# A hybrid decoder layer: conv states as whole tiles, the mLSTM's maps in three fp32r passes, five background steps beside the first norm

## The chip, the cores and the metric

The kernel runs on one core of a Trainium2 chip. The metric is device time in microseconds (us) of one execution. TensorE (PE) does the matrix products, with its weight loads shown apart as PEld; VectorE (DVE), ScalarE (ACT) and GpSimd (POOL) do the rest, and SyncE (SP) issues most of the DMAs. ACT issues some DMAs as well. Each engine works through its own list of instructions in order.

## The reference, cut to what matters

```
z = x @ w_in            # q, k, v, c (mLSTM's q/k path), vm, o, i, f
c_act = silu(causal_conv(c, w_conv, b_conv))             # width 4, depthwise
q = einsum('nlhd,hde->nhle', c_act, w_mq)                # 4 heads of 128: the "maps"
k = einsum('nlhd,hde->nhle', c_act, w_mk) * 128 ** -0.5
att = swa_attend(...)                                    # window 128, sinks, ALiBi
h = mlstm_chunk(C, n, m, q, k, v, logi, logf)            # chunk after chunk of 128 tokens
y = concat([head_norm(att), head_norm(sigmoid(o) * h)])
x1 = layer_norm(ALPHA * x + y @ w_out)                   # the "first norm"
out = layer_norm(ALPHA * x1 + (silu(x1 @ w_gate) * (x1 @ w_up)) @ w_down)
```

There are 2048 prompt tokens with 16 meta tokens ahead of them, and 8 running sequences of 8 tokens (the sample), 2128 columns in all. For the sample the conv begins with three stored columns of each sequence (state_conv, `sconv` in the kernel). The last three c columns of the prompt and of each sequence are outputs (`pconv`, `osconv`). Model width is 1024, and everything is float32.

## The kernel before, in words

Tokens lie along the free axis of a tile and features along the partitions. An accurate product is three fp32r matmuls: a tensor is split into a high part (a cast, `hi_of`, L111) and the rest (a subtraction, L120), and `mm3` multiplies high by high, high by low and low by high (L123, L124, L125). One output tile takes 8 slices of the inner dimension, so 24 matmuls.

Stage 1a (up to about 228 us) makes v, vm, o and the gates. Stage 1b (228 to about 505 us) goes over five groups of columns, `IN_GROUPS`, 426 columns wide (the last one 424). In each group nine weight tiles `m` follow one another: first the four of c, then those of q and k. Three of them (`late`) are left out of the last group and done in stage 2. A c tile is copied to `ext` (L969), the conv runs on ACT and DVE (L923 to L929) and gives `cz`, and four tiles later `maps` multiplies it with two 128x128 matrices (L937); the result goes through `ev` (L939) to FM in DRAM. These L937 matmuls take plain float32 operands. In the last group the sample's columns have a tile `exs` of their own, into which three stored columns are loaded (L973, once a head), and out of which three columns are stored (L976); L975 stores the prompt's three. All of these are issued by ACT.

In the first group the weights of stage 1b come through a raw tile `wbr`, of which there is one, and `mapr` has a tile of its own.

Stage 2 (505 us to the end) takes five groups of `FF_GROUPS` columns: `out_proj` (weights by `wtile`, L1000, three ahead at most; inputs by `load_y`, L1047), `ln1`, then gate, up and down products and the second norm. Ahead of the first group `load_z` (L1058) loads the residual, and the tiles `xr` for the late products come by L1186. The first `ln1` sums squares (L450), forms 1/sqrt on DVE (`rsqrt`, L129 to L136, a chain of small instructions), spreads it by matmul (L462), scales (L1106), and makes the high and low parts of x1 (L1115, L1122).

Attention and mLSTM of the chunks are *background steps*: `bg_step()` takes the next step of a generator, and `pace` spreads steps over the other work. The first norm has 12 steps of its own, behind `mark[7]`, the last L1122 of the norm: `tc.issue_after` keeps their instructions on an engine behind that one in order of issue. The order of instructions within each engine is otherwise decided by a scheduler. PSUM has 3 buffers named `gps` and 5 named `bps`.

Of the kernel before, what the change touches and what calls it, by code (L numbers as in the profile page):

```python
# [9 lines left out]
F32 = mybir.dt.float32  # L10
F32R = mybir.dt.float32r
# [6 lines left out]
KD = 8  # L18
# [31 lines left out]
def tile_hymba(  # L50
# [5 lines left out]
    nc = tc.nc  # L56
    V, A, G, PE, SP = nc.vector, nc.scalar, nc.gpsimd, nc.tensor, nc.sync
# [17 lines left out]
    def gps(shape=None):  # L75
        return pg.tile(shape or [128, 512], F32, tag="g", name="gps")
# [32 lines left out]
    def hi_of(eng, out, src):  # L109
        if eng == "a":  # L110
            A.copy(out, src)  # L111
        elif eng == "p":
            G.tensor_scalar(out=out, in0=src, scalar1=1.0, scalar2=0.0, op0=ALU.mult, op1=ALU.add)
        else:
            V.tensor_copy(out, src)

    def split(eng, hi, lo, src, veng=V):

        hi_of(eng, hi, src)
        return veng.tensor_tensor(out=lo, in0=src, in1=hi.bitcast(F32), op=ALU.subtract)  # L120

    def mm3(out, wh, wl, xh, xl, start, stop):
        PE.matmul(out, lhsT=wh, rhs=xh, start=start, stop=False)  # L123
        PE.matmul(out, lhsT=wh, rhs=xl, start=False, stop=False)  # L124
        PE.matmul(out, lhsT=wl, rhs=xh, start=False, stop=stop)  # L125
# [34 lines left out]
    def load_w(i):  # L160
        m = MT[i]
        if i < NEARLY:
            raw = ep.tile([128, KD, 128], F32, tag="wbr", name="wbr", bufs=1)
            hi, lo = w_tile(), w_tile()
        else:
            raw = b1["w"].tile([128, KD, 128], F32, tag="wbr", name="wbr", bufs=1)
            hi = b1["w"].tile([128, KD, 128], F32R, name=f"wbh{m}")
            lo = b1["w"].tile([128, KD, 128], F32R, name=f"wbl{m}")
        SP.dma_start(out=raw, in_=w1b[:, m, :].rearrange("p (k j) -> p k j", j=128))
        split("p" if i % 2 else "a", hi, lo, raw)  # L170
        wbh[m], wbl[m] = hi, lo
# [10 lines left out]
    with ExitStack() as s1:  # L182
        wp = s1.enter_context(tc.tile_pool(name="w1a", bufs=1, reuse_waits="tile"))
# [44 lines left out]
        start = [[f() for _ in CUT] for f in (gps, bps)]  # L228
# [14 lines left out]
        for i in range(NCH + 1):  # L243
# [11 lines left out]
            else:  # L255
                ps = []
                for c0, w in CUT:
                    xh, xl, n = xs[i]
                    p = (gps if flip[0] % 8 < 3 else bps)()
# [586 lines left out]
    for c in range(NCH):  # L846
        e = P0 + 128 * (c + 1)
# [8 lines left out]
    def bg_step():  # L856
        while done[0] < len(queue) and queue[done[0]][1] <= ready[0]:
            try:
                next(queue[done[0]][3])
                return True  # L860
            except StopIteration:
                done[0] += 1
        return False
# [7 lines left out]
    def steps_to(col):  # L871
        return sum(q[2] for q in queue[done[0]:] if q[0] <= col)
# [31 lines left out]
    with ExitStack() as s1:  # L904
        wp = s1.enter_context(tc.tile_pool(name="w1b", bufs=1, reuse_waits="tile"))
        b1.update(w=wp)
        tp = s1.enter_context(tc.tile_pool(name="t1b", bufs=1, reuse_waits="tile"))
        mapr = wp.tile([128, 8, 128], F32, name="mapr")
        ext = {}
        for g, w in enumerate(IN_GROUPS):  # L910
            c0 = sum(IN_GROUPS[:g])
            wp_ = w if g < 4 else w - NS

            def conv(h):

                e, es = ext[g, h]
                z = tp.tile([128, 426], F32, tag="cz", name="cz", bufs=CZ)
                th = tp.tile([128, 426], F32, tag="ct", name="ct", bufs=1)
                runs = [(z[:, 0:wp_], lambda j: e[:, j:j + wp_])]
                if es is not None:  # L920
                    runs.append((z[:, wp_:w].rearrange("p (n i) -> p n i", i=8), lambda j: es[:, :, j:j + 8]))
                for o, src in runs:
                    A.activation(out=o, in_=src(0), func=AF.Identity, scale=Q[:, Q_WC + 4 * h:Q_WC + 4 * h + 1],  # L923
                                 bias=Q[:, Q_BC + h:Q_BC + h + 1])
                    for j in range(1, 4):
                        V.scalar_tensor_tensor(out=o, in0=src(j), scalar=Q[:, Q_WC + 4 * h + j:Q_WC + 4 * h + j + 1],
                                               in1=o, op0=ALU.mult, op1=ALU.add)
                A.activation(out=th[:, 0:w], in_=z[:, 0:w], func=AF.Tanh, scale=0.5)
                V.scalar_tensor_tensor(out=z[:, 0:w], in0=th[:, 0:w], scalar=1.0, in1=z[:, 0:w],  # L929
                                       op0=ALU.add, op1=ALU.mult)  # L930
                return z

            def maps(h, cc):
                for j in range(2):
                    p = gps()
                    m = 4 * j + h
                    PE.matmul(p[:, 0:w], lhsT=mapr[:, m, :], rhs=cc[:, 0:w], start=True, stop=True)  # L937
                    ev = tp.tile([128, 426], F32, tag="ev", name="ev", bufs=4)
                    A.activation(out=ev[:, 0:w], in_=p[:, 0:w], func=AF.Copy,  # L939
                                 scale=0.5 if j == 0 else 0.5 * 128.0 ** -0.5)  # L940
                    A.dma_start(out=FM[:, 5 + 4 * j + h, c0:c0 + w], in_=ev[:, 0:w])

            conved = {}
            for idx, m in enumerate(MT[:NMT[g]]):
                if g == 0 and NEARLY <= idx + 3 < len(MT):
                    load_w(idx + 3)
                if g == 0 and idx == 3:
                    SP.dma_start(out=mapr, in_=wmap)
                if g == 1 and idx == 3:
                    with tc.issue_after(xdma[0].ins):  # L950
                        SP.dma_start(out=skT[:, :, 0:120], in_=ckT[:, :, 8:128])
                        SP.dma_start(out=sv[0:120], in_=cv[8:128])
                if g == 0 and idx == 2:
                    gates()
                p = gps()
                for k in range(KD):
                    xh, xl = xg[g, k]
                    mm3(p[:, 0:w], wbh[m][:, k, :], wbl[m][:, k, :], xh[:, 0:w], xl[:, 0:w], k == 0, k == KD - 1)
                if m < 5:
                    out_q(tp, p, m, c0, w)  # L960
                else:
                    h = m - 5
                    e = tp.tile([128, 429], F32, tag="ext", name="ext", bufs=5)
                    if g == 0:
                        V.memset(e[:, 0:3], 0.0)
                    else:
                        pw = IN_GROUPS[g - 1]
                        V.tensor_copy(e[:, 0:3], ext[g - 1, h][0][:, pw:pw + 3])
                    A.copy(e[:, 3:3 + wp_], p[:, 0:wp_])  # L969
                    es = None  # L970
                    if g == 4:
                        es = tp.tile([128, 8, 11], F32, tag="exs", name="exs", bufs=4)
                        A.dma_start(out=es[:, :, 0:3], in_=sconv[:, h])  # L973
                        A.copy(es[:, :, 3:11], p[:, wp_:w].rearrange("p (n i) -> p n i", i=8))
                        A.dma_start(out=pconv[:, h, :], in_=e[:, wp_:wp_ + 3])  # L975
                        A.dma_start(out=osconv[:, h], in_=es[:, :, 8:11])  # L976
                    ext[g, h] = (e, es)
                    conved[h] = conv(h)
                if idx - MDLY in conved:
                    maps(idx - MDLY, conved.pop(idx - MDLY))  # L980
                left = sum(NMT[g:]) - LEFT - idx
                if g > 0:
                    pace(steps_to(need(0)) / max(left, 1.0))
            for h in sorted(conved):
                maps(h, conved.pop(h))
            if g + 1 < 5:
                for k in range(KD):
                    load_xg(g + 1, k)
            ready[0] = c0 + w if g < 4 else c0
            if g == 0:  # L990
                early.close()
                bp = ctx.enter_context(tc.tile_pool(name="bg", bufs=1, side="right", reuse_waits="tile"))


    with ExitStack() as s2:
# [184 lines left out]
        cl, wl_ = sum(IN_GROUPS[:4]), IN_GROUPS[4]  # L1180
# [12 lines left out]
        mark = {7: None}  # L1193
        for _ in ln1(z, FF_GROUPS[0], s0, x1, True, mark):
            pass
        for m in late:
            h, l = wnext()
            p = bps()
# [1 line left out]
                mm3(p[:, 0:wl_], h[:, k, :], l[:, k, :], xq[k][0][:, 0:wl_], xq[k][1][:, 0:wl_], k == 0, k == KD - 1)  # L1200
            out_q(None, p, m, cl, wl_)
        ready[0] = T
        with tc.issue_after(mark[7]):
            for _ in range(12):
                bg_step()
        pend = None
        for g in range(NG):
            w = FF_GROUPS[g]
# [161 lines left out]
```

## Time and profile before

| | |
|---|---|
| three runs | 2504.2, 2506.12, 2508.94 us (median 2506.12) |
| the profiled execution | 2508.94 us, of which the span of its instructions is 2507.1 us |
| PE busy | 98% of the span |
| DVE, ACT, POOL busy | 60%, 38%, 13% |
| DMA | 327.89 MB, 197330 packets, of them 31010 under 512 B |

The page cuts the span in 40 slices of 63 us and gives the busy share of each engine in tenths. PE is at 9 in all but four of them, and its granted clock at 9 (90% or more of full speed) in all but two. Such a view shows which engine bounds the whole; the few places at which PE stands still are seen in the timeline alone.

### The profile page before, as it was taken

The page shows a single profiled execution, that of the slowest core. Times are in us where ns is not written, and L with a number is a line of the kernel's source. Part 1 is how long each engine was busy: PE and PEld are TensorE (multiplying, and loading weights), DVE is VectorE, ACT ScalarE, POOL GpSimd, SP SyncE. Part 2 cuts the span into 40 slices and gives each one's busy share as a digit, 9 for nine tenths or more (in the row PEclk, how much of TensorE's full clock was granted, in tenths as well). Part 3 has the DMA queues.
Part 4 walks back from the last instruction along what each step waited for, and adds up shares of the span by engine and source line. Part 5 has one row for each costly group of instructions (what it writes and reads, how often), then busy time and mean ns, then how long its engine had stood idle before and what let it go on. Part 6 is the DMA issues. An engine that isn't in the chain of part 4 may idle for free.

```text
span 2507.1 us, 34929 instructions
## 1 busy us (share of the span) xinstructions
PE 2444.7 (98%) x13135; PEld 2267.2 (90%) x13135; DVE 1514.9 (60%) x3129; ACT 955.3 (38%) x1730; POOL 328.3 (13%) x253
## 2 busy tenths in 40 slices
PE   8999999889999999999999999999999999999997
PEld 8999888788989989888999899989899999999997
DVE  6214466457786888656674976666775434764444
ACT  3112444335433444324333543343343323443332
POOL 1000000021000014210011500100420000420001
PEclk9999999998999999999999999999999999999998
DMA  7222534563444543554343353433344333343342
GB/s 234 89 90 85 173 119 131 132 207 117 144 130 126 160 146 94 175 159 144 120 137 121 106 188 122 140 119 107 109 142 133 117 111 121 104 143 114 118 127 77
DMA packets 197330, 327.89 MB, mean 131 GB/s; under 512 B 31010, under 2 KB 133498, under 8 KB 197146
## 3 DMA queue, kind: packets, MB, share of 16 engines
q1 hardware_dynamic: 170400, 294.29, 38.7%
q10 hardware_dynamic: 26762, 31.36, 3.6%
q8 instruction: 104, 1.70, 0.3%
q14 instruction: 64, 0.52, 0.1%
HBM read 281.59 MB, written 44.99 MB: 130 GB/s over the span
## 4 chain that ended last, share of the span: by engine, by line
PE 88%; DVE 4%; DMA 4%; ACT 1%; issue 1%; POOL 0%; SPq 0%; ACTq 0%; DVEq 0%; POOLq 0%
PE gps L123 25%; PE gps L125 24%; PE gps L124 24%; PE bps L123 2%; PE bps L125 2%; PE bps L124 2%; DMA w<-in_wo 1%; PE bps L513 1%; PE bps L549 1%; PE bps L542 1%; PE gps L937 1%; DVE w L120 1%; PE bps L682 1%; PE bps L655 1%; PE bps L672 1%
## 5 line engine op out<-in xcount | busy, mean ns | idle before, releaser
L123 PE MATMUL gps<-x,w 128*128 128x440 f32 (+4 forms) x2240 | 792.3, 358 | 11.1 <-DVE z L1075 5.6
L125 PE MATMUL gps<-x,w 128*128 128x440 f32 (+4 forms) x2240 | 797.9, 357 | 3.4 <-POOL w L120 2.7
L124 PE MATMUL gps<-x,w 128*128 128x440 f32 (+4 forms) x2240 | 794.0, 356 | 0.6 <-DVE x L1122 0.6
L111 ACT CAST w<-w 128x1024 fp32r<-128x1024 f32 (+2 forms) x423 | 400.6, 947 | 775.2 <-DMA w<-in_wd 271.8
L120 DVE TENSOR_TENSOR w<-w 128x1024 fp32r<-128x1024 f32 (+2 forms) x391 | 441.5, 1130 | 359.7 <-ACT w L111 185.4
L123 PEld LDWEIGHTS gps<-x,w 128*128 128x128 f32 x2240 | 422.4, 189 | 36.5 <-DVE z L1075 7.4
L125 PEld LDWEIGHTS gps<-x,w 128*128 128x128 f32 x2240 | 422.6, 189 | 23.3 <-POOL w L120 4.4
L124 PEld LDWEIGHTS gps<-x,w 128*128 128x128 f32 x2240 | 422.6, 189 | 18.4 <-DVE x L1122 0.9
L123 PE MATMUL gps<-hh,w 128*128 128x440 f32 (+2 forms) x880 | 314.8, 362 | 1.4 <-DVE z L1172 1.3
L125 PE MATMUL gps<-hh,w 128*128 128x440 f32 (+2 forms) x880 | 313.1, 357 | 0.0
L124 PE MATMUL gps<-hl,w 128*128 128x440 f32 (+2 forms) x880 | 312.5, 356 | 0.0
L123 PEld LDWEIGHTS gps<-hh,w 128*128 128x128 f32 x880 | 166.1, 189 | 11.9 <-issue 4.6
L124 PEld LDWEIGHTS gps<-hl,w 128*128 128x128 f32 x880 | 166.3, 189 | 8.1 <-issue 1.5
L125 PEld LDWEIGHTS gps<-hh,w 128*128 128x128 f32 x880 | 166.1, 189 | 7.4 <-issue 0.5
L120 POOL TENSOR_TENSOR w<-w 128x1024 fp32r<-128x1024 f32 x32 | 77.4, 2419 | 727.1 <-ACT w L111 475.2
L1172 DVE SCALAR_TENSOR_TENSOR z<-z,gps 128x440 f32<-128x440 f32 (+2 forms) x160 | 93.0, 589 | 69.1 <-PE gps L125 68.7
L111 ACT CAST hh<-hr 128x440 fp32r<-128x440 f32 (+2 forms) x110 | 60.0, 545 | 165.2 <-DVE hr L1158 165.0
L1158 DVE SCALAR_TENSOR_TENSOR hr<-ft,gps 128x440 f32<-128x440 f32 (+2 forms) x110 | 64.9, 590 | 81.3 <-PE gps L125 81.0
L1155 ACT ACTIVATE ft<-gps 128x440 f32<-128x440 f32 (+2 forms) x110 | 57.4, 522 | 113.1 <-PE gps L125 112.6
L120 DVE TENSOR_TENSOR hl<-hr,hh 128x440 fp32r<-128x440 f32 (+2 forms) x110 | 83.8, 762 | 27.6 <-ACT hh L111 27.3
L1066 POOL TENSOR_TENSOR zs<-zs,z 128x440 f32<-128x440 f32 (+2 forms) x58 | 80.0, 1379 | 102.0 <-DVE z L1075 66.3
L1156 DVE SCALAR_TENSOR_TENSOR ft<-ft,gps 128x440 f32<-128x440 f32 (+2 forms) x110 | 64.7, 588 | 46.4 <-ACT ft L1155 46.3
(338 smaller groups left out, 3111.0 us busy)
## 6 DMA issues: line engine op xcount, KB each, us to landing
w<-in_wg SPq DMA_DIRECT2D x110, 512.0 KB, 3.5
w<-in_wu SPq DMA_DIRECT2D x110, 512.0 KB, 3.5
w<-in_wd SPq DMA_DIRECT2D x80, 384.0 KB, 3.1
w<-in_wd SPq DMA_DIRECT2D x80, 320.0 KB, 2.9
w<-in_wo SPq DMA_DIRECT2D x40, 512.0 KB, 3.7
FM<-ev ACTq DMA_DIRECT2D x52, 213.0 KB, 1.9
TM<-st ACTq DMA_DIRECT2D x16, 578.0 KB, 3.7
vmo<-TM SPq DMA_DIRECT2D x16, 514.0 KB, 3.4
```

The costliest lines, as they stand in the source:

```text
L111: A.copy(out, src)
L120: return veng.tensor_tensor(out=lo, in0=src, in1=hi.bitcast(F32), op=ALU.subtract)
L123: PE.matmul(out, lhsT=wh, rhs=xh, start=start, stop=False)
L124: PE.matmul(out, lhsT=wh, rhs=xl, start=False, stop=False)
L125: PE.matmul(out, lhsT=wl, rhs=xh, start=False, stop=stop)
L513: PE.matmul(s[g][:, j, 0:nk], lhsT=x[r, 2 * tt + j, :], rhs=y[r, 0:nk], start=(i == 0), stop=(i == 2))
L542: PE.transpose(pt[0:n, 128 * t:128 * t + 128], Pt[:, 4 * g + t, c0:c0 + n], ident)
L1066: G.tensor_tensor(out=s[:, 0:w], in0=s[:, 0:w], in1=z[m][:, 0:w], op=ALU.add)
L1155: A.activation(out=t[:, 0:w], in_=pgt[:, 0:w], func=AF.Tanh, scale=0.5)
L1156: V.scalar_tensor_tensor(out=t[:, 0:w], in0=t[:, 0:w], scalar=1.0, in1=pgt[:, 0:w], op0=ALU.add, op1=ALU.mult)
L1158: V.scalar_tensor_tensor(out=hr[:, 0:w], in0=t[:, 0:w], scalar=0.5, in1=pu[:, 0:w], op0=ALU.mult, op1=ALU.mult)
L1172: V.scalar_tensor_tensor(out=zm, in0=zm, scalar=ALPHA if s == 0 else 1.0, in1=p[:, 0:w], op0=ALU.mult, op1=ALU.add)
```

## The change

1. *Conv states.* The four loads of `sconv` become one DMA into a tile `cvi` (issued by SP in group 1), and the sample's and the prompt's last columns are gathered by DVE copies in `cvo` and `cvp`, which two SP DMAs store after the last head. Twelve DVE copies are added; twelve ACT DMAs go, three SP DMAs come.
2. *Maps.* `mapr` is loaded through the shared raw tile and split in `maph` and `mapl`; `cz` is split in two tiles `cs` (three buffers for all), and `mm3` replaces the plain matmul. `ct` has two buffers.
3. *Background steps.* Five of the 12 steps at the first norm are no longer kept behind `mark[7]`.
4. A scratch size of the DMA's is set when the program is made.

```
-        mapr = wp.tile([128, 8, 128], F32, name="mapr")
+        maph = wp.tile([128, 8, 128], F32R, name="maph")
+        mapl = wp.tile([128, 8, 128], F32R, name="mapl")
+        cvi = tp.tile([128, 4, 8, 3], F32, name="cvi")
+        cvo = tp.tile([128, 4, 8, 3], F32, name="cvo")
+        cvp = tp.tile([128, 4, 3], F32, name="cvp")
...
-                th = tp.tile([128, 426], F32, tag="ct", name="ct", bufs=1)
+                th = tp.tile([128, 426], F32, tag="ct", name="ct", bufs=2)
...
+                ch, cl = (tp.tile([128, 426], F32R, tag="cs", name="cs", bufs=3) for _ in range(2))
+                split("a", ch[:, 0:w], cl[:, 0:w], cc[:, 0:w])
...
-                    PE.matmul(p[:, 0:w], lhsT=mapr[:, m, :], rhs=cc[:, 0:w], start=True, stop=True)
+                    mm3(p[:, 0:w], maph[:, m, :], mapl[:, m, :], ch[:, 0:w], cl[:, 0:w], True, True)
...
                 if g == 0 and idx == 3:
+                    mapr = wp.tile([128, KD, 128], F32, tag="wbr", name="mapr", bufs=1)
                     SP.dma_start(out=mapr, in_=wmap)
+                    split("a", maph, mapl, mapr)
                 if g == 1 and idx == 3:
                     with tc.issue_after(xdma[0].ins):
+                        SP.dma_start(out=cvi, in_=sconv)
...
-                        A.dma_start(out=es[:, :, 0:3], in_=sconv[:, h])
+                        V.tensor_copy(es[:, :, 0:3], cvi[:, h])
                         A.copy(es[:, :, 3:11], p[:, wp_:w].rearrange("p (n i) -> p n i", i=8))
-                        A.dma_start(out=pconv[:, h, :], in_=e[:, wp_:wp_ + 3])
-                        A.dma_start(out=osconv[:, h], in_=es[:, :, 8:11])
+                        V.tensor_copy(cvp[:, h, :], e[:, wp_:wp_ + 3])
+                        V.tensor_copy(cvo[:, h], es[:, :, 8:11])
+                        if h == 3:
+                            SP.dma_start(out=pconv, in_=cvp)
+                            SP.dma_start(out=osconv, in_=cvo)
...
-        with tc.issue_after(mark[7]):
-            for _ in range(12):
+        for i in range(12):
+            if i < 5:
                 bg_step()
+            else:
+                with tc.issue_after(mark[7]):
+                    bg_step()
```

The line numbers of the changed kernel are 13 higher from stage 2 on: L1000 is L1013 there, L1047 is L1060, L1058 is L1071, L1106 is L1119, L1122 is L1135, L1186 is L1199.

SP's list around the start of out_proj (`in_wo` are its weights, YD its inputs, `z` and `xr` the loads named above). Before:

```order
L1047 DMA x<-YD 128x384 x2
L1000 DMA w<-in_wo 128x1024
L1047 DMA x<-YD 128x384
L1000 DMA w<-in_wo 128x1024 x2
...
L1058 DMA z<-in_xT 128x384 x5
L1186 DMA xr<-in_xT 128x424
L1058 DMA z<-in_xT 128x440 x5
L1000 DMA w<-in_wo 128x1024
```

And of the change:

```order
L1013 DMA w<-in_wo 128x1024
L988 DMA out_pconv<-cvp 128x12
L1013 DMA w<-in_wo 128x1024
L989 DMA out_osconv<-cvo 128x96
...
L1071 DMA z<-in_xT 128x384 x4
L1071 DMA z<-in_xT 128x440
L1199 DMA xr<-in_xT 128x424
L1013 DMA w<-in_wo 128x1024
L1071 DMA z<-in_xT 128x440 x5
```

The two stores of conv states now stand between the second, the third and the fourth of the weight loads, and the fifth weight load has one of the next group's `z` loads (440 wide) right ahead of it instead of five.

DVE's list in the first norm, from the instruction that starts the 1/sqrt (L455) to the one that ends it. Before:

```order
L455 TENSOR_SCALAR rs<-gps 128x3
L129 TENSOR_SCALAR rs<-rs 128x3
L131 TENSOR_SCALAR rs<-rs 128x3
L120 TENSOR_TENSOR w<-w 128x1024
L134 TENSOR_TENSOR rs<-rs 128x3
```

And of the change (L518 and L523 are attention's scores and their maximum, L676 is the mLSTM's state):

```order
L455 TENSOR_SCALAR rs<-gps 128x3
L120 TENSOR_TENSOR w<-w 128x1024
L518 ISA P,mx<-bps,C,R 128x256
...
L131 TENSOR_SCALAR rs<-rs 128x3
L523 TENSOR_SCALAR mx<-mx 128x8
L524 TENSOR_TENSOR mx<-R,mx 128x8
L134 TENSOR_TENSOR rs<-rs 128x3
...
L676 SCALAR_TENSOR_TENSOR S<-S,DEC,bps 128x129
```

Four L518, L523, L524, two L676 and a copy (L572) have moved in between the steps of the 1/sqrt; before, all of them stood behind the last L1122. On PE the list has changed too, ahead of L462:

```order
L450 MATMUL gps<-avg,sq 128x1 x5
L513 MATMUL bps<-kt,qt 128x256 x2
L672 MATMUL bps<-wkv,ktm 128x129 x2
L682 MATMUL bps<-S,qs 128x129
L683 MATMUL bps<-vmo,gm 128x129
L682 MATMUL bps<-S,qs 128x129
L683 MATMUL bps<-vmo,gm 128x129
L462 MATMUL gps<-C,rs 128x128 x3
```

Before, L462 stood right behind the five L450; the attention and mLSTM matmuls between them came later.

## Rows read from the trace of the kernel before

**Rows 1.** The page: engines' share of the span, and the chain that ended last.

```profile
PE 2444.7 (98%) x13135; PEld 2267.2 (90%) x13135; DVE 1514.9 (60%) x3129; ACT 955.3 (38%) x1730; POOL 328.3 (13%) x253
...
PE 88%; DVE 4%; DMA 4%; ACT 1%; issue 1%; POOL 0%; SPq 0%; ACTq 0%; DVEq 0%; POOLq 0%
```

**Rows 2.** Windows: length; PE, PEld, DVE, ACT, POOL busy; granted clock, DMA share, GB/s.

```profile
300.00:450.00 150.00, 150.00 (x814) 129.02 (x813) 105.41 (x310) 72.87 (x181) 5.79 (x6) 1.00 0.39 122
486.00:498.20 12.20, 5.97 (x24) 5.75 (x25) 3.69 (x7) 4.42 (x8) 0.00 (x0) 0.72 0.84 113
522.00:531.00 9.00, 6.33 (x28) 5.70 (x27) 3.94 (x5) 4.48 (x6) 1.38 (x2) 0.81 0.79 301
561.00:579.00 18.00, 10.55 (x45) 9.29 (x44) 12.97 (x37) 12.19 (x21) 4.03 (x4) 0.62 0.12 41
```

**Rows 3.** Timeline of PE around one pair of maps in group 1: start, duration, what.

```profile
306.16 0.36 PE L123 MATMUL gps<-x,wbh 128*128 128x426 f32 x1
...
307.14 0.36 PE L125 MATMUL gps<-x,wbl 128*128 128x426 f32 x1
307.33 1.59 PE L937 MATMUL gps<-cz,mapr 128*128 128x426 f32 x4
...
308.96 0.36 PE L124 MATMUL gps<-x,wbh 128*128 128x426 f32 x1
```

**Rows 4.** Groups of instructions in stage 1b: busy, mean ns of one, idle before.

```profile
L111 ACT CAST x<-x 128x426 fp32r<-128x426 f32 x21 | 11.3, 548 | 21.9 <-DMA x<-in_xT 17.1 <-DMA FM<-ev 4.3 <-ACT ev L887 0.4
...
L120 DVE TENSOR_TENSOR x<-x 128x426 fp32r<-128x426 f32 x22 | 13.0, 600 | 28.4 <-ACT x L111 14.4 <-PE gps L124 13.9
```

**Rows 5.** Timeline of ACT and PE in group 0.

```profile
241.26 1.05 ACT L111 CAST wbh<-wbr 128x1024 fp32r<-128x1024 f32 x1 [0.79 <-DMA wbr<-in_w1b]
...
251.16 1.59 PE L937 MATMUL gps<-cz,mapr 128*128 128x426 f32 x4
...
253.19 1.05 ACT L111 CAST wbh<-wbr 128x1024 fp32r<-128x1024 f32 x1 [0.25 <-DMA wbr<-in_w1b]
```

**Rows 6.** DMA from 470 to 500 us: packets, and issues (median us to landing).

```profile
DMA packets 5917, 3.04 MB, mean 101 GB/s; under 512 B 4856, under 2 KB 5410, under 8 KB 5916
...
w<-in_wo SPq DMA_DIRECT2D x4, 512.0 KB, 18.5
```

**Rows 7.** The page: the same weight load over the whole run.

```profile
w<-in_wo SPq DMA_DIRECT2D x40, 512.0 KB, 3.7
```

**Rows 8.** Timeline, ACT and PE, end of stage 1b (brackets: idle, releaser).

```profile
490.62 1.04 ACT L111 CAST w<-w 128x1024 fp32r<-128x1024 f32 x1 [6.95 <-DMA w<-in_wo]
...
492.23 0.72 PE L123 MATMUL gps<-x,wbh 128*128 128x424 f32 x1 [6.81 <-ACT ev L887]
...
498.21 1.59 PE L937 MATMUL gps<-cz,mapr 128*128 128x424 f32 x4
...
504.47 0.66 PE L123 MATMUL gps<-x,w 128*128 128x384 f32 x1
```

**Rows 9.** Timeline of SP and PE in the first out_proj; its chain.

```profile
515.28 2.38 SPq L1058 DMA_DIRECT2D z<-in_xT  x5
...
517.80 5.99 DMA w<-in_wo
...
524.97 0.44 PE L123 MATMUL gps<-x,w 128*128 128x384 f32 x1 [2.03 <-ACT w L111]
```

**Rows 10.** Timeline of DVE and PE in the first norm.

```profile
562.05 0.16 DVE L455 TENSOR_SCALAR rs<-gps 128x3 f32<-128x3 f32 x1 [1.42 <-PE gps L450]
...
565.45 1.65 PE L462 MATMUL gps<-C,rs 128*128 128x128 f32 x6 [3.44 <-DVE rs L136]
...
575.99 0.48 DVE L518 CUSTOM_DVE_ANT_0 P<-bps,C,R 128x256 f32<-128x256 f32 x1
...
576.39 0.48 DVE L518 CUSTOM_DVE_ANT_0 P<-bps,C,R 128x256 f32<-128x256 f32 x1
...
581.38 0.61 DVE L676 SCALAR_TENSOR_TENSOR S<-S,DEC,bps 128x129 f32<-128x129 f32 x2 [2.61 <-PE bps L672]
```

More of the change, by code (lines that the diff above doesn't have):

```diff
@@ L1336 @@
     from concourse.bass_utils import run_bass_kernel_spmd as _run
-    nc = _bacc.Bacc("TRN2", target_bir_lowering=False, num_devices=1)
+    nc = _bacc.Bacc("TRN2", target_bir_lowering=False, num_devices=1, dynamic_dma_scratch_size=1024)
     lay = _layout(inputs)
```

## The prediction

> **What bounds the kernel now.** I read the page first: PE is busy in 98% of the span and holds 88% of the chain that ended last, DMA and DVE 4% each [rows 1]. So there are two ways to be faster: less work on PE, or fewer of the places at which PE stands still or runs at a low clock. Work added on another engine costs something only where it makes PE wait.
>
> The windows show where that is [rows 2]. From 300 to 450 us PE is busy for all of 150.00 us at clock 1.00, while DVE has 105.41 and ACT 72.87 of 150: the loop over groups is bound by PE alone. From 486 to 498.2 us PE is busy for 5.97 of 12.20 us at a granted clock of 0.72; from 522 to 531 us for 6.33 of 9 at 0.81; in the first norm, from 561 to 579 us, for 10.55 of 18 at 0.62. A mean under 1 is time at 1.2 GHz instead of 2.4, and it comes here behind PE's idle time each time.
>
> The timeline then says what PE waited for. At 492.23 us it had been idle for 6.81 us, and the releaser is an ACT eviction [rows 8]. But ACT itself had been idle for 6.95 us in front of a weight cast at 490.62 that waited for a load of out_proj's weights: ACT works in order, and the eviction stood behind that cast. So the wait is a late DMA. The DMA view of 470 to 500 us shows how late: four such loads took 18.5 us in the median to land, against 3.7 us for the 40 of the whole run [rows 6, 7]. In the same 30 us 5917 packets moved only 3.04 MB, and 4856 of them were under 512 B [rows 6]. These are the conv states' stores, 12 bytes a run.
>
> **The change part by part.** The sum is made against the profiled execution, 2508.94 us (span 2507.1 and 1.84 around it). It is the slowest of the three runs; the median, 2506.12, is 2.82 lower.
>
> *A. Maps on PE.* A matmul of 426 columns issues every (307.14 - 306.16)/5 = 0.196 us [rows 3]. From 307.14 to 308.96 lie one matmul, the pair of maps (four records) and one more matmul: 1.82 - 2 x 0.196 = 1.43 us for the pair. Six fp32r matmuls in its place take 1.18, which saves 0.25. Groups 0 to 3 have 16 pairs: -4.1 us; the last group is counted in C. The bounds are -2 (each set of three starts with a hand-over that costs half the saving) and -4.1.
>
> The Trainium skill ("FP8 and Floating Point Precision", section "TensorE Precision Notes") says that true FP32 takes four passes through the array. By that a pair would hold eight passes, 1.57 us by the step above, and A would be -6.3. The trace differs, 1.43 us, and decides.
>
> The split adds on ACT a cast of 0.55 us and on DVE a subtraction of 0.60 us for each of 20 heads [rows 4]. Four of each in a group of about 48 us are hidden by idle time: DVE has 44.6 us of 150 free there, ACT 77 [rows 2]. Without that cover it would be at most 20 x 0.60 = 12 us.
>
> *B. Group 0.* `mapr` now takes a turn in the raw weight tile. From the cast at 241.26 to that at 253.19 there are two turns [rows 5], 6.0 us each. The maps' weights take the turn after 241.26: cast at 247.2, low part 2.3 us later (1.05 and about 1.2), ready at 249.5, and the first map stands at 251.16. That is a margin of 1.7 us. The weights behind it come 6 us later and are needed later still. What can stick is the order on DVE: the gates' small chain now stands behind a subtraction that waits for a buffer, and PE has a matmul of that chain behind the first maps. Bounds: 0, and 3 us (two subtractions and a pair, 2 x 0.60 + 1.18, with hand-overs). I take +1.5.
>
> *C. End of stage 1b.* If the twelve ACT DMAs are why the weights are late, PE loses neither the 6.81 us [rows 8] nor the half-rate stretch behind it: 24 matmuls took 498.21 - 492.23 = 5.98 us instead of 4.70. That is -8.1. The last three pairs of maps took 504.47 - 498.21 = 6.26 us [rows 8]. Afterwards they take 3 x (1.18 + 0.60 and a hand-over of some 0.2) = 5.9, since with three `cs` buffers a head's subtraction waits for the maps of the head before: -0.4. On the other side ACT does four casts of 0.55 there that it did not do, in front of evictions that PE waits for, and the third weight load now stands on SP behind the prompt's store, which waits for the last head's copies, so that its cast (1.05) comes among the evictions as well: +3.3 if none of it is hidden. I take -5. Bounds: -2 (the loads come only some us sooner) and -8.5.
>
> The skill speaks against this part in one point: "DMA: Bandwidth & Descriptors", section "Specifications", wants at least 512 B in a transfer for full rate, with a read-modify-write below that, and the whole-tile stores still have only 48 and 384 B a partition. By it they stay slow, and C would be nearer to its -2. The trace agrees that such packets are slow together (101 GB/s in the 30 us above), and no run here shows what one costs.
>
> *D. First out_proj.* The fifth weight load is issued at 517.80, right behind five `z` loads of the next group that take SP 2.38 us [rows 9], and lands 5.99 later (3.7 in the median [rows 7]). PE idles 2.03 us for it [rows 9], and in the 9 us from 522 it idles 2.67 in all at a clock of 0.81 [rows 2], another (1 - 0.81) x 9 = 1.7 us: 4.4. With one `z` load ahead instead of five it is issued 4/5 x 2.38 = 1.9 earlier, and with less traffic up to 2.3 us sooner to land. I take -3.5; bounds 0 (other transfers fill the gap) and -4.4.
>
> *E. First norm.* PE idles 3.44 us in front of L462, during the 1/sqrt [rows 10]. DVE's steps between L455 and its end now have four L518 (0.40 apart), two L676 (0.61 together [rows 10]) and three small ones of about 0.15 among them: 1.6 + 0.61 + 0.45 = 2.7 us later. PE fills some of that with matmuls that it would do later, and the work moved comes off the stretch behind. Bounds: -1 and +4 (the eight L532 ahead of the last L1122, too). I take +1.5.
>
> The single loads of `sconv` delay nothing on PE today, and of the second half of stage 2 only the order changes: 0, and 2 either way.
>
> Sum: -4.1 + 1.5 - 5 - 3.5 + 1.5 = -9.6. That is 2499.3 by the profiled execution and **2496.5 us** by the median.
>
> **The rivals.**
>
> 1. *The waits go almost whole.* The loads land in 4 us, ACT's casts hide, the norm costs nothing: -4.1 + 0.5 - 8.5 - 4.4 + 0 = -16.5, 2489.6. For it speaks that ACT is idle for 6.95 us in front of that cast; against it, that ACT's and SP's order get longer by the change itself.
> 2. *The late weights do not come from the small packets.* Twice 512 KB of weights, inputs and residual are loaded at that time too, and the DMA share stands at 0.84 [rows 2]. If that volume is what holds the loads, C and D are -1 together, and -4.1 + 1.5 - 1 + 1.5 = -2.1: 2504, the same within what can be measured. Against it: 3.04 MB in 30 us is 101 GB/s [rows 6], while from 522 to 531 us the same engines move 301 [rows 2].
> 3. *Slower: DVE stands behind PE.* DVE works in order, and a head's subtraction may wait until PE has done the maps before. A weight tile takes 24 x 0.196 = 4.7 us, of which DVE has about 30% free, 1.4 us. A wait beyond 1.4 us makes the next conv or input split late, and then PE stands. With a wait of 2.4 us at 16 heads: +16 - 9.6, 2512.5; it decides from a wait of about 2 us on (+9.6). Against it: the maps of two heads lie a whole weight tile apart in groups 0 to 3, so the buffer is free long before.
> 4. *The norm takes it.* The 1/sqrt and what follows come 2.7 later, PE's clock stays low longer, and it costs +6 instead of +1.5: 2501, faster by the bound still, but barely.
>
> **How the numbers follow.** Chances: the forecast 0.46 (2492 to 2501), rival 1 0.18, rival 2 0.18, rival 3 0.09, rival 4 0.09. A measurement of this kernel tells about 0.2%, 5 us, from no change, so *faster* is under 2501.1 and *slower* over 2511.1. Faster: 0.46 x 0.95 + 0.18 + half of rival 4 + a little of rival 2 = 0.44 + 0.18 + 0.05 + 0.04, about 0.71. Slower: most of rival 3 and a part of rival 2, 0.09. Same: 0.20. The range goes from 2487 (rival 1 with 3 us more) to 2507 (rival 2 with 3 more); it leaves out rival 3 and the edges.
>
> **What would show it.** A: a pair of maps in group 1 takes about 1.2 us between the matmuls around it. B: PE shows no idle time over 1 us before 300 us. C: the weight loads between 470 and 500 us land in about 4 to 6 us, the idle time of 6.81 is gone, and out_proj starts about 7.6 us earlier than at 504.47 (A, B and C). D: in the first out_proj no wait of PE for a weight over 1 us, clock 1.00. E: L462 begins about 6 instead of 3.4 us after L455. I am wrong if the loads still take over 10 us without the small packets, if DVE shows idle time in front of the subtractions of `cs` in groups 1 to 3 with PE idle behind it, or if later stages lose what these stretches win.

## The result, and the profile after

The change takes 2493.93 us in the median of five runs (2491.22 to 2495.77) against 2508.94 for the kernel before beside it (2504.2 to 2512.17): a ratio of 0.9947, 95% interval [0.9935, 0.9960]. By the ratio it is faster by some 13 us. The time lies within the stated range, 2.6 us under the forecast; the sum of -9.6 came to -13.1 between the two profiled executions, but two terms of that size are in it that the sum did not have.

The page of the change:

```profile
span 2494.0 us, 35048 instructions
PE 2438.8 (98%) x13175; PEld 2271.9 (91%) x13175; DVE 1519.9 (61%) x3162; ACT 965.2 (39%) x1751; POOL 331.5 (13%) x253
...
DMA packets 188866, 327.88 MB, mean 131 GB/s; under 512 B 22546, under 2 KB 125034, under 8 KB 188682
...
w<-in_wo SPq DMA_DIRECT2D x40, 512.0 KB, 3.8
```

PE is as busy a share of the span as before [rows 1], with 5.9 us less work in it. There are 8464 packets fewer for the same bytes.

The DMA view from 470 to 500 us, to be read beside [rows 6]:

```profile
DMA packets 3354, 5.80 MB, mean 193 GB/s; under 512 B 621, under 2 KB 2840, under 8 KB 3352
...
w<-in_wo SPq DMA_DIRECT2D x4, 512.0 KB, 4.6
...
out_osconv<-cvo SPq DMA_DIRECT2D x1, 48.0 KB
out_pconv<-cvp SPq DMA_DIRECT2D x1, 6.0 KB, 2.1
```

621 packets under 512 B instead of 4856, 193 GB/s instead of 101, and the weights land in 4.6 us instead of 18.5. PE's timeline at the end of stage 1b, to be read beside [rows 8]:

```profile
483.84 0.46 PE L123 MATMUL gps<-x,wbh 128*128 128x424 f32 x1 [0.32 <-ACT ev L887]
...
490.57 0.88 PE L123 MATMUL gps<-cs,maph 128*128 128x424 f32 x2 [1.07 <-ACT ev L946]
...
495.16 0.66 PE L123 MATMUL gps<-cs,maph 128*128 128x424 f32 x2 [0.67 <-ACT cs L111]
...
496.67 0.33 PE L123 MATMUL gps<-x,w 128*128 128x384 f32 x1
```

Idle times of 0.32, 1.07 and 0.67 us (and two under 0.4) stand where 6.81 stood, and the first matmul of out_proj (the last row) comes at 496.67 instead of 504.47. ACT's timeline shows what the 1.07 is:

```profile
488.26 0.51 ACT L111 CAST x<-x 128x384 fp32r<-128x384 f32 x1
489.05 1.05 ACT L111 CAST w<-w 128x1024 fp32r<-128x1024 f32 x1 [0.27 <-DVE cz L934]
490.00 0.94 ACT L946 ACTIVATE ev<-gps 128x424 f32<-128x424 f32 x2
```

PE waits there for an eviction (L946), and that stands on ACT behind a weight cast of 1.05 us.

A set of three passes in group 1 looks like this on PE:

```profile
315.95 0.36 PE L123 MATMUL gps<-cs,maph 128*128 128x426 f32 x1
...
316.93 0.36 PE L125 MATMUL gps<-cs,mapl 128*128 128x426 f32 x1
```

Six matmuls issue from 315.95 to 316.93 + 0.20, 1.18 us, as the sum had it against the 1.43 of the pair [rows 3].

In the first out_proj, PE and then SP:

```profile
519.61 0.45 PE L125 MATMUL gps<-x,w 128*128 128x384 f32 x1 [1.06 <-DVE w L120]
```

```profile
505.62 0.33 SPq L1013 DMA_DIRECT2D w<-in_wo  x1
...
511.62 0.33 SPq L1013 DMA_DIRECT2D w<-in_wo  x1
```

The fifth weight load is issued at 505.62, 8.95 us after out_proj began, against 13.33 before (517.80 [rows 9] less 504.47 [rows 8]). PE no longer waits for it, but for the sixth, 1.06 us, and its clock stays at 1.00.

The first norm, DVE and then PE, beside [rows 10]:

```profile
549.96 0.16 DVE L455 TENSOR_SCALAR rs<-gps 128x3 f32<-128x3 f32 x1 [3.11 <-PE gps L450]
...
551.21 0.48 DVE L518 CUSTOM_DVE_ANT_0 P<-bps,C,R 128x256 f32<-128x256 f32 x1
...
553.64 0.34 DVE L676 SCALAR_TENSOR_TENSOR S<-S,DEC,bps 128x129 f32<-128x129 f32 x1
...
555.01 0.16 DVE L136 SCALAR_TENSOR_TENSOR rs<-rs 128x3 f32<-128x3 f32 x1
```

```profile
552.64 0.71 PE L672 MATMUL bps<-wkv,ktm 128*128 128x129 f32 x4 [2.40 <-DVE mx L518]
...
555.22 1.63 PE L462 MATMUL gps<-C,rs 128*128 128x128 f32 x6 [0.21 <-DVE rs L136]
...
561.33 0.66 PE L123 MATMUL gps<-x,w 128*128 128x384 f32 x1 [2.50 <-DVE z L1119]
```

From L455 to L462 it is 5.26 us instead of 3.40. PE fills part of that with the matmuls that were moved (the row of 552.64 is one), but waits 2.40 us for L518 to free a buffer.

Cut at events that both traces have, the span comes apart as follows (the first matmul of the maps, the last group's first, the first of out_proj, the mean of the sums L1085 or L1098 as the norm begins, L462, and the same mean in the next group). The last column is a second profile of the change, taken later, less the same profile of before:

| stretch | before | after | difference | my terms | again |
|---|---|---|---|---|---|
| start to the first map | 251.16 | 251.42 | +0.26 | 0 | +0.52 |
| to the first map of the last group | 232.67 | 231.55 | -1.12 | A, B: -2.6 | -1.25 |
| to out_proj | 20.64 | 13.70 | -6.94 | C: -5 | -5.58 |
| first out_proj | 39.87 | 35.80 | -4.07 | D: -3.5 | -3.32 |
| to L462 | 21.11 | 22.75 | +1.64 | E: +1.5, with the next row | +1.91 |
| L462 to the next group's norm | 391.90 | 382.21 | -9.69 | | -11.47 |
| to the end of the span | 1549.75 | 1556.57 | +6.82 | 0 | +3.89 |

The cuts that no row shown so far has are these, of before:

```profile
483.83 1.58 PE L937 MATMUL gps<-cz,mapr 128*128 128x424 f32 x4
...
544.34 0.81 PE L1085 MATMUL gps<-zs,avg 128*128 128x384 f32 x2
...
957.35 0.90 PE L1085 MATMUL gps<-zs,avg 128*128 128x440 f32 x2
```

and of the change:

```profile
251.42 0.36 PE L123 MATMUL gps<-cs,maph 128*128 128x426 f32 x1
...
482.97 0.55 PE L123 MATMUL gps<-cs,maph 128*128 128x424 f32 x2
...
532.47 0.81 PE L1098 MATMUL gps<-zs,avg 128*128 128x384 f32 x2
...
937.43 0.90 PE L1098 MATMUL gps<-zs,avg 128*128 128x440 f32 x2
```

Up to L462 the differences add up to -10.2, near the -9.6 of the forecast. What I had not seen is the stretch behind it, and that the rest of the kernel can take 7 us more or less.

### The profile page after: what moved, and what is told of

The parts are those of the page before. It is cut to its first block, busy times and chain, and to the rows that moved or that the text cites. A ratio compares the mean times of both kernels' runs of the same rounds, so it can differ in the third digit from the quotient of the medians.

```text
span 2494.0 us, 35048 instructions
## 1 busy us (share of the span) xinstructions
PE 2438.8 (98%) x13175; PEld 2271.9 (91%) x13175; DVE 1519.9 (61%) x3162; ACT 965.2 (39%) x1751; POOL 331.5 (13%) x253
## 4 chain that ended last, share of the span: by engine, by line
PE 86%; DVE 6%; DMA 4%; ACT 1%; issue 1%; POOL 0%; SPq 0%; ACTq 0%; DVEq 0%
PE gps L123 24%; PE gps L124 24%; PE gps L125 24%; PE bps L123 2%; PE bps L125 2%; PE bps L124 2%; PE bps L513 1%; PE bps L549 1%; PE bps L542 1%; DVE w L120 1%; DMA w<-in_wo 1%; DMA w<-in_wd 1%; DMA out_oS<-P 1%; PE bps L655 1%; PE bps L682 1%
## 5 line engine op out<-in xcount | busy, mean ns | idle before, releaser
L120 DVE TENSOR_TENSOR w<-w 128x1024 fp32r<-128x1024 f32 (+2 forms) x391 | 442.4, 1132 | 352.1 <-ACT w L111 175.3
L120 POOL TENSOR_TENSOR w<-w 128x1024 fp32r<-128x1024 f32 x32 | 77.0, 2407 | 765.2 <-ACT w L111 620.2
L120 DVE TENSOR_TENSOR hl<-hr,hh 128x440 fp32r<-128x440 f32 (+2 forms) x110 | 82.9, 754 | 30.8 <-ACT hh L111 30.4
```

## The experiments

All were timed in five rounds or more; ratios are to the kernel before on the same chip, with 95% intervals. Theory: the small packets of `osconv` hold the weight loads, and that is most of it. Rivals: the volume that is loaded there anyway; the number and the place of the DMAs on ACT's list; the maps or the steps as the source of the gain.

### One part at a time

*Conv states alone:* the kernel before with the edits to `cvi`, `cvp` and `cvo` alone, `mapr` and its matmul as before.

> Only the conv states as whole tiles (part 1); maps and background steps as before. Packets theory: the weight loads at 470 to 500 us land in about 5 us instead of 18.5, PE's idle time of 6.8 us is gone, out_proj starts about 7 us earlier, and the time falls by 6 to 9 us. Volume theory: the loads still land after 10 us or more, and the time stays within 2 us. The five z loads still stand ahead of the fifth weight load here, so if their order is what made PE wait in the first out_proj, that wait of about 2 us stays.

2499.18 us, ratio 0.9957 [0.9943, 0.9971]. The DMA view from 470 to 500 us:

```profile
DMA packets 2598, 4.70 MB, mean 157 GB/s; under 512 B 537, under 2 KB 2084, under 8 KB 2596
...
w<-in_wo SPq DMA_DIRECT2D x4, 512.0 KB, 4.6
```

The packets theory agrees: 4.6 us to landing. (Twelve ACT DMAs are gone here as well; the next part separates the two.) From the last group's first map to out_proj it takes 10.98 us, a gain of 9.7. In the first out_proj the wait for the fifth weight shrinks from 2.03 to 1.00 us although the five `z` loads are still ahead of it, so their order is at most half of that wait; in later kernels with the same order it is 0.32 us (the stores without gaps) and none (those and the steps), apart from some 0.65 for that weight's low part, which all of these have.

*Maps alone:* `maph`, `mapl`, `cs` and `mm3`, conv states and steps as before.

> Only the maps in three fp32r passes (part 2); conv states and background steps as before. By the matmul steps: 16 pairs at 0.25 us saved and 1 to 1.5 us lost in group 0, so -2 to -4 us, with the late weights still there (18 us to landing, PE idle 5 to 7 us near 490 us). If the splits on ACT and DVE cost PE something, 0 or slower.

2516.06 us, ratio 1.0022 [1.0013, 1.0031]: slower. The miss is mine: with the late weights still there (15.4 us to landing), the last group's first map to out_proj takes 22.60 us instead of 20.64, and PE waits 2.41 us right ahead of it. In stage 1b it waits 8.1 us in three pieces, 4.9 the longest, for the eviction L887 on ACT, and 3.8 in two for the casts of `cs`.

*Steps alone:*

```
-        with tc.issue_after(mark[7]):
-            for _ in range(12):
+        for i in range(12):
+            if i < 5:
                 bg_step()
+            else:
+                with tc.issue_after(mark[7]):
+                    bg_step()
```

> Only the five background steps moved ahead (part 3). My step E: 1/sqrt of the first norm takes 2.7 us longer, +1.5 us on the whole. Rival: the work moved comes off a later stretch, where the profile of the change has PE idle 2.7 us less and no low clock between 733 and 761 us, so -4 to -8 us.

2507.72 us, ratio 0.9987 [0.9978, 0.9995]. The rival is nearer, but by less than it said: the norm up to L462 takes 25.09 us (+4.0), and from L462 to the next group's norm 381.17 (-10.7).

### Packets, or the number of DMAs

*Each head's store from a tile without gaps.* As many DMAs, by the same engine, in the same places:

```
-                        A.dma_start(out=osconv[:, h], in_=es[:, :, 8:11])
+                        co = tp.tile([128, 8, 3], F32, tag="co", name="co", bufs=4)
+                        V.tensor_copy(co, es[:, :, 8:11])
+                        A.dma_start(out=osconv[:, h], in_=co)
```

> The kernel before with as many DMAs from the same engine, but each head's osconv goes through a DVE copy into a tile without gaps: 96 bytes a partition instead of eight runs of 12, so 512 packets instead of 4096 for the four heads. If the number of packets delays the weights: landing falls from 18.5 to under 8 us, PE's idle time near 490 us falls by 4 us or more, -5 to -8 us. If the number of DMAs or their place on ACT's list does it, or the volume: within 2 us of before.

2496.86 us, ratio 0.9950 [0.9938, 0.9963]: this edit of three lines gives about all that the whole change gives. (Like the change, it sets the DMA's scratch size, as do all kernels here but that of the steps alone. The maps alone have this setting and the old stores, and the weights still take 15.4 us there, so it is not the cause.) The same view:

```profile
DMA packets 4219, 5.81 MB, mean 194 GB/s; under 512 B 1486, under 2 KB 3705, under 8 KB 4217
...
w<-in_wo SPq DMA_DIRECT2D x4, 512.0 KB, 5.0
...
out_pconv<-ext ACTq DMA_DIRECT2D x4, 1.5 KB, 4.0
out_osconv<-co ACTq DMA_DIRECT2D x4, 12.0 KB, 3.5
```

*Half of it:* the same for heads 1 and 3 alone.

> As e4_packets, but only for heads 1 and 3; heads 0 and 2 still store eight runs of 12 bytes a partition, so 2304 packets from osconv instead of 4096 (512 in e4_packets), with as many DMAs. If the delay grows with the packets that stand ahead of the weights: landing of the weights 8 to 13 us, PE idle 1 to 4 us near 490 us, -6 to -11 us. If a few such stores suffice to block: as before. If half of them is harmless: as e4_packets, -13.

2500.86 us, ratio 0.9984 [0.9974, 0.9993]. DMA, then PE:

```profile
DMA packets 5333, 4.82 MB, mean 161 GB/s; under 512 B 3199, under 2 KB 4819, under 8 KB 5331
...
w<-in_wo SPq DMA_DIRECT2D x4, 512.0 KB, 9.4
```

```profile
488.54 0.46 PE L123 MATMUL gps<-x,wbh 128*128 128x424 f32 x1 [2.41 <-ACT ev L887]
```

4096, 2304 and 512 packets of `osconv` give 18.5, 9.4 and 5.0 us to landing, and 6.81, 2.41 and 0 us of PE's idle time in front of that m tile. The other two profiles with 4096 packets have 13.1 (the steps alone) and 15.4 us (the maps alone) to landing. The delay grows with the packets. From the last group's first map to out_proj it takes 13.65 us, between 20.64 and 10.92. The whole time fell by less than I expected of it (0.9984, some 4 us, instead of 6 to 11): a miss, which the traces leave open. It was timed in another set of runs, with the kernel before at 2504.29 us, where the set of the stores without gaps had it at 2511.0.

### The change without one part

*Without the maps* (conv states and steps):

> The change without its maps: conv states as whole tiles and five background steps ahead, maps as plain float32 matmuls. If the maps in three passes are worth what the matmul steps say (about 4 us less on PE, 1 to 2 lost in group 0), this is 2 to 3 us slower than the change, ratio to before 0.9955 to 0.996. If they lose at the end of stage 1b what they save before (the change needs 13.7 us from its last pairs of maps to out_proj, the conv states alone 11.0), it is as fast or 1 to 2 us faster: 0.994 to 0.995.

2492.08 us, ratio 0.9921 [0.9907, 0.9934], faster than either expectation. And once more, beside the change itself:

> The change once more, beside the next three on the same chip: ratio to before 0.993 to 0.996.

> The change without its maps, once more, on the same chip as the change. If the maps in three passes lose about what they win (stage 1b: 245.3 us from the first map to out_proj in the change, 243.9 without them), it is as fast as the change or up to 5 us faster: 0.992 to 0.995. If they win 2 us or more as I had forecast, it is slower than the change by that.

The change: 2492.24 us, 0.9943 [0.9931, 0.9955]. Without its maps: 2492.03, 0.9942 [0.9926, 0.9959]. The maps in three passes are worth nothing that can be measured here.

*Without the steps* (conv states and maps; `if i < 0` in place of `if i < 5`):

> The change without its background steps: all 12 stay behind the last L1122 of the first norm. If the five steps are worth the 3 us that they gave alone, the ratio to before is about 0.996 to 0.9965. If my step E (+1.5 us for them) were right, it is 1.5 us faster than the change: 0.994. The 1/sqrt of the first norm should be unbroken again, L462 3.4 us after L455.

2503.59 us, ratio 0.9963 [0.9951, 0.9976]. L462 comes 3.43 us behind L455 again. Against 0.9943 and 0.9947 of the change the steps are worth some 4 us here, and 3 alone.

The larger part of what they save is seen at one place. PE in this kernel, then its window, and the window of the change from 25 us behind L462 to the next norm:

```profile
731.12 0.30 PE L743 MATMUL bps<-C,P 128*128 128x128 f32 x1 [2.19 <-DVE P L741]
```

```profile
724.00:752.00 28.00, 25.30 (x132) 23.17 (x130) 20.28 (x39) 9.36 (x19) 2.88 (x1) 0.88 0.49 143
```

```profile
580.22:937.43 357.21, 354.84 (x2092) 328.18 (x2091) 280.48 (x694) 151.87 (x322) 33.12 (x24) 1.00 0.46 142
```

A matmul of the sample's attention (L743) waits 2.19 us for DVE, and behind it the granted clock falls to 0.88 in the mean of 28 us: (1 - 0.88) x 28 = 3.4 us more. This wait, 1.9 to 2.2 us, stands in all six profiles without the steps (before and the five kernels with 12 steps behind the norm), and in none of the eight with them.

What makes DVE late is one instruction, and the one that POOL runs beside it. DVE and POOL without the steps, then DVE in the change:

```profile
728.57 2.40 DVE L741 TENSOR_SCALAR P<-P,mx 128x192 f32<-128x192 f32 x1
```

```profile
727.98 2.88 POOL L120 TENSOR_TENSOR w<-w 128x1024 fp32r<-128x1024 f32 x1 [26.01 <-DVE pt L134]
```

```profile
713.87 0.31 DVE L741 TENSOR_SCALAR P<-P,mx 128x192 f32<-128x192 f32 x1
```

L741 takes 2.40 us where it begins during a weight's subtraction on POOL (L120), and ends 0.1 us behind it; elsewhere it takes 0.31 or 0.32. All six profiles without the steps have it so, and in the eight with them no such subtraction runs beside it. What the steps save here is that meeting.

### The end of stage 1b

*Six `cs` buffers* instead of three (`bufs=6`):

> The change with six cs buffers instead of three, so that no head's subtraction waits for the maps of the head before. If that wait makes the end of stage 1b slow: from the first map of the last group to out_proj 11 to 12 us instead of 13.7, about 2 us faster than the change. If ACT's order does it (casts of cs and of weights ahead of the evictions), 13 us or more and no difference.

2495.95 us, ratio 0.9934 [0.9921, 0.9946]: 13.18 us there instead of 13.70, with one head's last four matmuls of the maps behind the first of out_proj. The buffers are not it. PE waits 1.64 us for L946 and 1.49 for a cast of `cs`, both on ACT, so ACT's list is what is left; no run moves the casts alone off ACT.

*Plain matmuls in the last group alone*, three passes in the other four, with `mapr` loaded again into the raw tile in group 1:

```
+                        mapr2[0] = wp.tile([128, KD, 128], F32, tag="wbr", name="mapr2", bufs=1)
+                        SP.dma_start(out=mapr2[0], in_=wmap)
...
+                    if g < 4:
                         mm3(p[:, 0:w], maph[:, m, :], mapl[:, m, :], ch[:, 0:w], cl[:, 0:w], True, True)
+                    else:
+                        PE.matmul(p[:, 0:w], lhsT=mapr2[0][:, m, :], rhs=cc[:, 0:w], start=True, stop=True)
```

> The change with maps in three passes in groups 0 to 3 alone; in the last group they are plain float32 matmuls, out of a second load of the maps into the raw weight tile. If the splits cost 2.7 us in the last group, as the two traces read beside each other say, stage 1b ends 2 to 3 us sooner than in the change and the kernel is 2 to 3 us faster (ratio 0.993 to 0.994). If not, the same as the change.

2495.74 us, ratio 0.9933 [0.9920, 0.9945]. The stretch takes 10.68 us, 3 less than in the change, as expected; from the first map to out_proj it is 241.48 us, the shortest of all (245.25 in the change, 243.85 without maps). The whole time does not show it: the ratio is that of the six-buffer kernel beside it, and 1557.1 us from the second group's norm to the end take it back.

### The smallest edits together

*The stores without gaps and the five steps:*

> The kernel before with each head's osconv stored from a tile without gaps (as in e4_packets) and the five background steps ahead; conv loads, prompt stores and maps as before. Packets theory and additive steps: as fast as the change without its maps or a little faster, ratio 0.990 to 0.993. If the whole-tile DMAs were worth more than the packets: 0.995 or more.

2488.98 us, ratio 0.9932 [0.9919, 0.9945], against 2492.24 for the change on the same chip: the lowest median of that chip, though the intervals of the ratios overlap.

## Why the prediction was right

**C, the late weights.** Right in its mechanism and under-sized: -6.94 for -5. Undoing the small packets alone gives -9.7 in that stretch, above my bound for all of it, and the packets are shown to be the cause by the same DMAs with fewer of them (18.5, 9.4, 5.0 us). Even the stores without gaps have runs of 96 bytes only; the Trainium skill ("DMA: Bandwidth & Descriptors", section "Specifications") wants 512 B in a transfer for full rate, and by that I had seen C nearer to -2. The runs don't bear out that consequence: with such stores the weights land in 5.0 us. The number of packets and their length change together here, and no run separates them. The +3.3 that I set against it for ACT's list was near: the splits cost 13.70 - 10.98 = 2.7 us there. In the second profile of the change it is 4.1 (15.06 - 10.97), as PE's clock falls behind a wait of 1.26 us, to a mean of 0.66 from 490.5 to 498.2 us. The hand-over of the three buffers, which I counted as well, was not what costs.

**A and B, the maps.** The step of 0.25 us a pair is right in group 1 and less so behind it: 64.78 to 63.74 us in group 1, 60.65 to 59.87 in group 2 and 51.07 to 50.58 in group 3, four pairs each, -1.04, -0.78 and -0.49. The failing step is "groups 0 to 3 have 16 pairs: -4.1"; why the saving shrinks is open. Group 0 takes 57.36 us instead of 56.17, +1.19 where I had -1.0 + 1.5. B's mechanism is there, the small chain's matmul that waits:

```profile
253.84 0.28 PE L386 MATMUL bps<-one,gsc 1*68 1x1 f32 x2 [1.09 <-DVE gsc L382]
```

But the other five profiles with the maps have 56.4 to 57.0 us in group 0, and those without them 56.2 to 56.9, so most of the 1.19 is this one profile. Together it is -1.12 for -2.6, and with 2.7 us lost in the last group the part is worth nothing, as the change without it shows. The 1.57 us that the prediction worked out for eight passes took a whole step of 0.196 for each; a pass inside one plain matmul need not take that, so the 1.43 of the rows does not decide against it.

**D, the first out_proj.** The size is near, -4.07 for -3.5, but the step "one `z` load ahead instead of five" is not shown to carry it. The fifth load is indeed issued 4.4 us sooner, and the wait moves on to the sixth. With the old order the stretch takes 37.53 and 36.62 us without the small packets, and 36.78 even with them, in the steps alone (where out_proj begins 8.3 us later); with the new order, in the change without its steps, 39.15, with a wait of 1.58 us. Two profiles of the change without its maps, which has the old order, differ by 2.0 us (37.27 and 39.23). So the 39.87 of before stands at the long end of what its order gives, and the size came out by luck in part. DMA is at a share of 0.79 to 0.89 from 8 to 28 us behind the start of out_proj in the profiles of before, the change, and the three kernels with 37.53, 36.62 and 39.15, and which weight comes last differs. The old 2.03 us cost more than its idle time, as PE's clock fell behind it; an idle time of 1.06 in the change did not bring that.

**E, the norm.** L462 comes 1.86 us later behind L455 than before, where I had 2.7, so +1.64 up to L462 agrees. It is so in the two profiles of the change alone: in the other six with the steps the stretch takes 24.5 to 25.2 us, 3.4 to 4.1 more than before, with attention's L542 ahead of L462 as well. What failed is "the work moved comes off the stretch behind" as a small item: that stretch gives 9.69 us. By the rows above some 5.6 of it are the wait of the sample's attention and the clock behind it (2.19 + 3.4). Some 2.5 are work that PE now does ahead of L462, where it is busy for 20.14 us instead of 17.67; the rest I did not locate.

**Later stages.** I gave them 0 and 2 either way; they took 6.82 more. Whether that is the change's is open. The same kernel (conv states and steps, without the maps) took 1556.3 us there in one profile and 1548.7 in another, on another chip. One place makes half of it, the fourth group's norm, in the first profile and in the second:

```profile
1771.53:1811.09 39.56, 37.02 (x188) 34.17 (x187) 34.17 (x50) 21.36 (x33) 22.00 (x15) 0.96 0.33 93
```

```profile
1770.17:1805.66 35.49, 35.48 (x188) 32.82 (x186) 31.37 (x50) 20.03 (x33) 22.39 (x15) 1.00 0.34 104
```

35.49 us or 39.56, by whether PE waits 2.54 us for the 1/sqrt and then runs at a lower clock, or does not wait at all. It is the meeting of DVE and POOL again, DVE and then POOL in the first profile:

```profile
1791.81 0.16 DVE L134 TENSOR_TENSOR rs<-rs 110x4 f32<-110x4 f32 x1
1792.01 2.31 DVE L135 SCALAR_TENSOR_TENSOR rs<-rs 110x4 f32<-110x4 f32 x1
```

```profile
1791.96 2.34 POOL L120 TENSOR_TENSOR w<-w 128x1024 fp32r<-128x1024 f32 x1 [1.39 <-PE gps L124]
```

A small instruction of the 1/sqrt, 0.16 us elsewhere, begins during the subtraction on POOL and ends with it; in the second profile the chain is done before POOL begins. This wait, 2.4 to 2.7 us, stands in all six profiles with the maps in three passes and in two of the eight without them (before and the one above). From the second group's norm to the end the six take 1551.3 to 1557.1 us, and seven of the eight 1547.8 to 1550.5. So the maps may well bring the loss, by when POOL and DVE meet; no run shows how.

Up to L462 the forecast is near by its places, with C above and A and B below their terms. Behind it the total came out near by luck: a gain that I had not seen, 9.69, met a loss of the later norms, 6.82. Of the signs that I had set, two were missed narrowly, PE's longest wait before 300 us in stage 1b (1.09 us instead of under 1) and that for a weight in out_proj (1.06), and the last one, that later stages lose what these stretches win, came half true.

## What to carry to other kernels

Read a late load by the packets that stand beside it, not by the bytes: here 48 KB in runs of 12 bytes held 512 KB loads for 18 us, and one copy into a tile without gaps, on an engine with time to spare, took that away. A saving on the engine that bounds a stretch is kept only as far as the engines that feed it are not the bound at the stretch's end; look at the last group by itself before splitting operands. When a small DVE instruction comes late, look at what POOL runs beside it. A short wait of PE should be priced with the clock behind it, and a small gain in one stage should be read at that stage, since later waits that come and go are of its size.

## What was not expected of the hardware

Some waits of PE cost more than themselves and others do not, and their length alone does not tell which. Behind waits of 2.03, 2.19 and 2.54 us (out_proj of before, the sample's attention, the fourth group's norm) the granted clock fell from 2.4 to 1.2 GHz for some microseconds; behind 1.06 us (the change, in out_proj) and 0.91 and 1.00 us (the conv states alone) it did not. Between these it went either way. In out_proj it fell behind 1.25 and 1.00 us in the six-buffer kernel and behind 1.17 and 0.65 in the change without its maps (second profile), and did not behind 1.28 and 0.64 with plain matmuls in the last group. At the end of stage 1b it fell behind 1.26 us in the second profile of the change and stayed at 1.00 behind 1.64 and 1.49 in the six-buffer kernel.

It was not expected either that a DVE instruction of 0.16 or 0.31 us can take as long as the weight's subtraction on POOL that runs beside it (2.3 to 2.9 us), nor that two profiles of one kernel differ by 7.6 us behind the second norm, half of it through such a meeting.
